# Two-input elementwise work moved from GpSimd to VectorE, high halves to ScalarE, in a hybrid attention layer

## Chip, cores and metric

The kernel runs on one core of a Trainium2 chip. The metric is device time in microseconds of one launch. TensorE, VectorE (DVE in the profile), ScalarE (ACT), GpSimd (POOL) and SyncE (SP, which issues the DMAs) each run their own instructions in order and wait for one another by semaphores.

## The reference, cut to what matters

One encoder layer over 2048 frames of 1024 features, in float32:

```python
h = layer_norm(x, ln_in_g, ln_in_b)
(aq, ak, av, ag, gq, gk, gv, gg, glr) = split(h @ w_in)
att = chunk_band_attention(aq, ak, av, rel_bias) * silu(ag)      # 8 heads x 64, 576-frame band
log_a = log_sigmoid(glr @ w_gla_gate + b_gla_gate) / 16
o = gla_chunked(gq, gk, gv, log_a)                               # 4 heads, dk 64, dv 128
gla = rms_normalised(o) * gla_norm_g * silu(gg)
r = alpha * h + concat(att, gla) @ w_out
r = r + sigmoid(r @ w_ple_gate + b_ple_gate) * (p @ w_ple)
out = layer_norm(r, ln_g, ln_b)
```

In the gated part, with `L` the running sum of `log_a` in a chunk of 64 frames, the kernel needs `q * exp(L)`, `k * exp(-L)`, `q * exp(-L)`, `k * exp(L)` and `k * exp(L_end - L)`.

## The kernel before

**Split operands.** Every large product is made of three matmuls: an operand is split into a high half (`hi`, the value rounded to the matmul's float32r) and a low half (`lo`, the value minus `hi`), and hi x hi, hi x lo and lo x hi are summed. So each of the 46 weight slabs used for the first time is loaded raw (128 x 1024, twice 128 x 1088), then split: a copy gives `whi`, a subtraction `wlo`. Halves that are used again in the second half of the sequence are stored to DRAM (`w_keep`, line 268) and fetched back. `ln_T` (line 220) splits the normalised, transposed input into `hh` and `hl`; `mix_split` (line 1133) splits the mixed heads into `mh` and `ml`. The helper `copy_split` (line 150) copies on VectorE and subtracts on an engine that its caller names.

**Stages.** The sequence is worked in two halves of 1024 frames (`sb`), each half in two groups of 512 (`g`). A half has a gated stage (`gla_phase`: projections and four gated units), an attention stage (`attn_phase`: four pairs of heads, 16 steps a pair and group) and an output stage (`out_phase`: output projection, embedding projection, gate, last normalisation). The second half has its weights fetched, so all weight splits are in the first half, between 10 and 611 us. The last normalisation of group 0 (`ln_out`) runs beside the gate's products; that of the second half's group 1 is `ln_last`.

**The order of the work** is written out by hand. `gemm` (line 302) issues 3 x 8 matmuls for one 128 x 512 result and calls `tick` after each four (after each eight in `gemm_v`). A tick runs what was put off to it: `defer(n, f)` puts `f` n ticks later in the list `pend`, or in `lazy` for weights. `set_side` adds a generator ("side") that is stepped beside the matmuls; each `yield w` lets `w` ticks pass, times the side's scale. `w_done(i)` (line 298) is called after the last matmul of weight i; one tick later `w_next(i + 4)` splits the weight four places on (high half on VectorE, low half on GpSimd) and starts the raw load two places further on. Raw weights have two buffers (three weights at the start have others), split ones eight, four weights' worth. Within what the dependencies allow, the framework lays out each engine's order; in the first stage (`head`, line 742) the order of VectorE, ScalarE and GpSimd is the program's own.

**The places the change touches.** `ln_T`: of the splits of full 512-column blocks, half have their subtraction on GpSimd (12 in all); the first group's half blocks have it on VectorE. `w_split` and `w_next` (lines 274 and 294): above. `ln_out` (line 370): per block of 128 frames two halves are scaled on VectorE (line 393) and get their bias added on GpSimd (line 395), 24 adds in all. `unit` (line 627), eight of them: after `gates` has made `eL`, `en`, `kd` and `kn`, VectorE makes `kd = kd * k`, GpSimd `qf`, and 1.5 ticks later TensorE transposes `kd` (line 639), ScalarE copies it out; VectorE makes `kn` in two steps (lines 642 and 645), GpSimd `qn` and `kf`. `head`: splits the first four weights in a written order. `mix_split`: 32 high halves on VectorE, the low halves half on VectorE and half on GpSimd. What stays on GpSimd in both kernels: the power in `rstd_of` (line 155), the scaling of the probabilities in `norm` (line 1002), `r_sum` (line 1191) and `ln_last`'s share.

Of the kernel before, what the change touches and what calls it, by code (L numbers as in the profile page):

```python
# [26 lines left out]
F32 = mybir.dt.float32  # L27
# [17 lines left out]
def hymba_layer_kernel(  # L45
# [174 lines left out]
    def ln_T(g, xs, pst, blocks=range(4)):  # L220
        c0 = blocks[0] * 128
        c = slice(c0, c0 + 128 * len(blocks))
        for k in range(8):
            ps = pst()
            for b in blocks:
                nc.tensor.transpose(ps[:, b * 128:(b + 1) * 128],
                                    xs[b][k // 4][:, (k % 4) * 128:(k % 4 + 1) * 128], ident)
            t = U("t")
            nc.scalar.activation(t[:, c], ps[:, c], AF.Identity, bias=lnb[:, k:k + 1], scale=lng[:, k:k + 1])
            if c0 == 0:  # L230
                hT_hi[k][g] = U("hh", F32R)
                hT_lo[k][g] = U("hl", F32R)
            copy_split(t[:, c], hT_hi[k][g][:, c], hT_lo[k][g][:, c],
                       nc.vector if k % 2 or len(blocks) < 4 else nc.gpsimd)
            yield
# [37 lines left out]

    def w_split(i, part=None):
        if i < len(order) and i not in wt and not first_use(i):
            w_fetch(i)
        if i not in wt or isinstance(wt[i], tuple) and len(wt[i]) == 2:
            return
        if part != "lo":
            raw = wt[i]  # L280
            hi = w_tile(pool_w, F32R, i, "whi")
            if part == "act":
                nc.scalar.activation(hi, raw, AF.Copy)
            else:
                nc.vector.tensor_copy(hi, raw)  # L285
            wt[i] = (raw, hi, None)
        if part in (None, "lo"):
            raw, hi, _ = wt[i]
            lo = w_tile(pool_w, F32R, i, "wlo")
            nc.gpsimd.tensor_tensor(lo, raw, hi.bitcast(F32), op=OP.subtract)  # L290
            wt[i] = (hi, lo)
            w_keep(i)

    def w_next(i):
        w_split(i)
        w_load(i + 2)

# [72 lines left out]
    def ln_out(sb, g, rows, ys, pst):  # L370
        for b in range(4):
# [20 lines left out]
            for hf in range(2):  # L392
                nc.vector.scalar_tensor_tensor(y[hf], y[hf], r[:, 0:1], rows[hf],  # L393
                                               op0=OP.mult, op1=OP.mult)
                nc.gpsimd.tensor_tensor(y[hf], y[hf], rows[2 + hf], op=OP.add)  # L395
                ln_put(sb, g, b, hf, y[hf])
# [110 lines left out]
    def gla_phase(sb):  # L507
# [119 lines left out]
        def unit(s, g, before):  # L627
# [6 lines left out]
            nc.vector.tensor_tensor(kd, kd, k, op=OP.mult)  # L634
            nc.gpsimd.tensor_tensor(qf, q, eL, op=OP.mult)
            yield 1.5
            p2 = ps_kv()
# [3 lines left out]
            nc.scalar.activation(kdT, p2, AF.Copy)  # L641
            nc.vector.tensor_tensor(kn[:, :, 0:3:2, :], c42(k), c42(en), op=OP.mult)
            nc.gpsimd.tensor_tensor(qn, q, en, op=OP.mult)
            yield 1.5
            nc.vector.tensor_tensor(kn[:, :, 1, :], kn[:, :, 1, :], c42(k)[:, :, 0, :], op=OP.mult)
            nc.gpsimd.tensor_tensor(kf, k, eL, op=OP.mult)
            yield 1.5

# [93 lines left out]
        def head(idx):  # L742
# [34 lines left out]
            with tc.manual_schedule(engines={E.DVE, E.Activation, E.Pool}):  # L777
# [10 lines left out]
                x_half(xs[1][1], r, nm, 0, nc.vector)  # L788
                w_split(0)
                for k, _ in enumerate(ln_T(0, xs, bank, range(0, 2))):  # L790
                    if k == 1:
                        w_split(1, "act")
                        w_split(1, "lo")
                w_split(2, "act")
# [338 lines left out]
    def mix_split(g):  # L1133
        for k in (4, 5, 0, 1, 2, 3, 6, 7):
# [3 lines left out]
            else:  # L1138
                ml[k][g] = U("ml", F32R)
            copy_split(mix[k][g], mh[k][g], ml[k][g], nc.gpsimd if k % 2 else nc.vector)  # L1140
            yield
# [208 lines left out]
```

## Time and profile before

| | |
|---|---|
| median of 3 runs | 1408.23 us (1406.45 to 1409.65) |
| the profiled execution | 1408.62 us |
| its span, first to last instruction | 1406.8 us |
| TensorE matmul | 96% of the span, 8440 matmuls |
| VectorE | 865.4 us, 62%, 1785 instructions |
| ScalarE | 552.3 us, 39%, 1126 instructions |
| GpSimd | 380.8 us, 27%, 355 instructions |
| mean granted clock of TensorE | 0.990 of full speed |
| DMA | 186.40 MB, 132 GB/s in the mean |

The span runs from the first instruction to the last; the execution's own time is 1.8 us longer. Matmuls follow one another in a pipeline, so a busy TensorE isn't one at its peak, but a gap in it is time in which no matmul ran. An engine's wait is put down to the instruction whose end released it. In a line of the time line, `[2.19 <-DVE hh L151]` means that the engine had been idle for 2.19 us and was released by VectorE's instruction of line 151 that writes `hh`.

### The profile page before, as it was taken

What the parts mean: (1) busy time and instruction counts of PE and PEld (TensorE: products, weight loads), DVE (VectorE), ACT (ScalarE), POOL (GpSimd) and SP (SyncE); (2) the same over time, 40 slices, a digit from 0 to 9 for tenths busy, and PEclk for the clock granted to TensorE, in tenths of its full rate; (3) what the DMA queues carried; (4) which work ended last, traced back from release to release, by engine and by line L of the source; (5) the groups of instructions that cost most, each with busy time, mean ns of one, the idle gap of its engine ahead of it and who ended that gap; (6) DMA issues with size and microseconds to landing.
All of it is one profiled execution on the core that took longest, in us unless ns stands there. A gap on an engine that the chain in (4) does not pass through costs nothing.

```text
span 1406.8 us, 22169 instructions
## 1 busy us (share of the span) xinstructions
PE 1348.1 (96%) x8440; PEld 1171.5 (83%) x8440; DVE 865.4 (62%) x1785; ACT 552.3 (39%) x1126; POOL 380.8 (27%) x355
## 2 busy tenths in 40 slices
PE   5879999999999999999999999999999999999985
PEld 5868888889988888788897888988998888888875
DVE  7674736666666976665875452666566668332286
ACT  4644414544454311414454542445454542112222
POOL 4251513232333432422462120121111123000052
PEclk9999999999999999999999999999999999999998
DMA  8360435241633335656613042421332213335551
GB/s 316 52 194 2 183 120 209 93 165 39 219 109 133 119 119 200 249 214 230 221 61 120 5 164 75 135 92 61 99 114 99 84 46 103 115 114 196 191 180 60
DMA packets 63442, 186.40 MB, mean 132 GB/s; under 512 B 7216, under 2 KB 9320, under 8 KB 63336
## 3 DMA queue, kind: packets, MB, share of 16 engines
q1 hardware_dynamic: 62816, 183.41, 37.1%
q10 hardware_dynamic: 520, 1.57, 1.0%
q8 instruction: 67, 1.10, 0.3%
q14 instruction: 39, 0.32, 0.1%
HBM read 119.28 MB, written 65.67 MB: 131 GB/s over the span
## 4 chain that ended last, share of the span: by engine, by line
PE 49%; DVE 6%; ACT 2%; issue 1%; POOL 1%; ACTq 0%; DVEq 0%; POOLq 0%
PE proj L313 32%; PE proj L912 3%; PE proj L553 3%; PE PV L1044 2%; PE PT L1024 2%; PE S L990 1%; PE S L988 1%; DVE t L1199 1%; DVE y L1205 1%; DVE ysb L393 1%; PE O L700 1%; DVE P L994 1%; DVE y L1207 0%; POOL ysb L395 0%; DVE bst L379 0%
## 5 line engine op out<-in xcount | busy, mean ns | idle before, releaser
L313 PE MATMUL proj<-hh,whi 128*128 128x512 f32 (+1 forms) x912 | 358.6, 393 | 0.3 <-DVE k L896 0.3
L313 PE MATMUL proj<-hh,wlo 128*128 128x512 f32 (+1 forms) x912 | 357.9, 392 | 0.0
L313 PE MATMUL proj<-hl,whi 128*128 128x512 f32 (+1 forms) x912 | 354.4, 389 | 0.0
L1006 POOL TENSOR_SCALAR P<-P,s 128x640 f32<-128x640 f32 (+4 forms) x128 | 96.0, 750 | 424.2 <-DVE s L1005 302.2
L313 PEld LDWEIGHTS proj<-hh,whi 128*128 128x128 f32 x912 | 172.9, 190 | 29.4 <-issue 1.0
L313 PEld LDWEIGHTS proj<-hl,whi 128*128 128x128 f32 x912 | 172.7, 189 | 29.6
L313 PEld LDWEIGHTS proj<-hh,wlo 128*128 128x128 f32 x912 | 172.7, 189 | 29.5
L998 ACT ACTIVATE P<-P,s 128x640 f32<-128x640 f32 (+4 forms) x128 | 97.6, 763 | 174.7 <-DVE s L997 150.9
L290 POOL TENSOR_TENSOR wlo<-wraw,whi 128x1024 fp32r<-128x1024 f32 (+1 forms) x46 | 111.3, 2418 | 134.4 <-DVE whi L285 78.3
L994 DVE CUSTOM_DVE_ANT_0 P<-S,bias 128x640 f32<-128x640 f32 (+4 forms) x128 | 94.5, 738 | 53.4 <-PE S L990 47.5
L1027 DVE TENSOR_TENSOR PTl<-PT,PTh 128x384 fp32r<-128x384 f32 (+2 forms) x232 | 102.4, 472 | 14.2 <-ACT PTh L1026 12.8
L313 PE MATMUL proj<-mh,whi 128*128 128x512 f32 x256 | 99.9, 390 | 0.0
L313 PE MATMUL proj<-mh,wlo 128*128 128x512 f32 x256 | 99.7, 389 | 0.0
L1026 ACT ACTIVATE PTh<-PT 128x384 fp32r<-128x384 f32 (+2 forms) x232 | 87.1, 421 | 27.4 <-PE PT L1024 26.3
L159 POOL TENSOR_TENSOR rstd<-v,nhalf 128x1 f32<-128x1 f32 (+2 forms) x44 | 35.6, 815 | 225.2 <-DVE v L157 224.5
L1024 PE MATMUL PT<-ident,P 128*128 128x128 f32 x560 | 84.1, 275 | 3.0 <-DVE PTl L1027 3.0
L553 PE MATMUL proj<-whi,hl 128*128 128x272 f32 (+1 forms) x256 | 76.5, 302 | 2.9 <-DVE hl L152 1.6
L553 PE MATMUL proj<-whi,hh 128*128 128x272 f32 (+1 forms) x256 | 75.5, 301 | 2.8 <-DVE hh L151 2.2
L313 PE MATMUL proj<-ml,whi 128*128 128x512 f32 x192 | 75.1, 391 | 0.0
L912 PE MATMUL proj<-whi,hh 128*128 128x256 f32 x256 | 74.3, 290 | 0.0
L1199 DVE SCALAR_TENSOR_TENSOR t<-t,ple 128x512 f32<-128x512 f32 (+1 forms) x36 | 39.8, 1107 | 53.2 <-ACT t L1198 53.1
L912 PE MATMUL proj<-wlo,hh 128*128 128x256 f32 x256 | 72.3, 282 | 0.0
(224 smaller groups left out, 2691.2 us busy)
## 6 DMA issues: line engine op xcount, KB each, us to landing
whi<-wkept SPq DMA_DIRECT2D x64, 512.0 KB, 3.7
wlo<-wkept SPq DMA_DIRECT2D x64, 512.0 KB, 4.5
wkept<-whi SPq DMA_DIRECT2D x44, 512.0 KB, 2.9
wkept<-wlo SPq DMA_DIRECT2D x44, 512.0 KB, 2.9
wraw<-in_wi_dram SPq DMA_DIRECT2D x26, 512.0 KB, 5.0
x<-in_x_dram SPq DMA_DIRECT2D x32, 256.0 KB, 5.8
out_dram<-ysb SPq DMA_DIRECT2D x32, 256.0 KB, 2.0
v<-vhist SPq DMA_DIRECT2D x24, 256.0 KB, 3.0
```

Of the source, the lines that this page charges most:

```text
L159: nc.gpsimd.tensor_tensor(r[:, :n], v1[:, :n], nhalf[:, :n], op=OP.pow)
L290: nc.gpsimd.tensor_tensor(lo, raw, hi.bitcast(F32), op=OP.subtract)
L313: nc.tensor.matmul(ps[:, cols], lhsT=l[:, c0 + k, :], rhs=rhs(k)[m][:, cols], start=(j == 0), stop=(j == n - 1))
L553: nc.tensor.matmul(ps[:, c0:c0 + nw], lhsT=h[k][g][:, b * 128:(b + 1) * 128], rhs=W[k // 4][m][:, k % 4, :], start=(n == 0), stop=(n == 23))
L912: nc.tensor.matmul(ps[:, bb * 256:bb * 256 + 256], lhsT=h[k][g][:, c], rhs=W[k // 4][m][:, k % 4, :], start=(k == 0 and n == 0), stop=(k = ...
L994: nc.vector.tensor_tensor_reduce(P[:, :ncol], ps[:, 512 - n_prev:512 + n_cur], bias[pr, h][:, 640 - ncol:640], 1.0, -3e38, OP.add, OP.max, ...
L998: nc.scalar.activation(P[:, :ncol], P[:, :ncol], AF.Exp, bias=s4[:, 1:2], scale=1.0, accum_out=s4[:, 2:3])
L1006: nc.gpsimd.tensor_scalar(P[:, :ncol], P[:, :ncol], s4[:, 3:4], 1.0, op0=OP.mult, op1=OP.mult)
L1024: nc.tensor.transpose(ps[:, b, :], P[:, (b0 + b) * 128:(b0 + b + 1) * 128], ident)
L1026: nc.scalar.activation(Th[:, ks, cs], ps[:, :nb, :], AF.Copy)
L1027: nc.vector.tensor_tensor(Tl[:, ks, cs], ps[:, :nb, :], Th[:, ks, cs].bitcast(F32), op=OP.subtract)
L1199: nc.vector.scalar_tensor_tensor(t, t, 1.0, ple[s][:, cols], op0=OP.add, op1=OP.mult)
```

## The change

GpSimd's subtractions and products with two tensor inputs in `ln_T`, `w_split`, `ln_out`, `unit` and `mix_split` go to VectorE. The high halves of weights, apart from the very first, and of the mixed heads are made on ScalarE. `w_next` makes the high half at once, and the low half and the next raw load two ticks later. In `unit` the transposes of `kd` come 2 ticks instead of 1.5 after its product, with `kn`'s two products issued in front of them and `qn` and `kf` behind. In `head` the first two low halves come after the splits of the first two blocks of input. The whole diff:

```diff
--- before.py
+++ after.py
@@ -231,7 +231,7 @@
                 hT_hi[k][g] = U("hh", F32R)
                 hT_lo[k][g] = U("hl", F32R)
             copy_split(t[:, c], hT_hi[k][g][:, c], hT_lo[k][g][:, c],
-                       nc.vector if k % 2 or len(blocks) < 4 else nc.gpsimd)
+                       nc.vector)
             yield
 
 
@@ -272,28 +272,32 @@
                 nc.sync.dma_start(d[n], w_flat(wt[i][n]))
 
     def w_split(i, part=None):
+
         if i < len(order) and i not in wt and not first_use(i):
             w_fetch(i)
         if i not in wt or isinstance(wt[i], tuple) and len(wt[i]) == 2:
             return
-        if part != "lo":
+        if not isinstance(wt[i], tuple):
             raw = wt[i]
             hi = w_tile(pool_w, F32R, i, "whi")
-            if part == "act":
+            if part == "dve":
+                nc.vector.tensor_copy(hi, raw)
+            else:
                 nc.scalar.activation(hi, raw, AF.Copy)
-            else:
-                nc.vector.tensor_copy(hi, raw)
             wt[i] = (raw, hi, None)
         if part in (None, "lo"):
             raw, hi, _ = wt[i]
             lo = w_tile(pool_w, F32R, i, "wlo")
-            nc.gpsimd.tensor_tensor(lo, raw, hi.bitcast(F32), op=OP.subtract)
+            nc.vector.tensor_tensor(lo, raw, hi.bitcast(F32), op=OP.subtract)
             wt[i] = (hi, lo)
             w_keep(i)
 
     def w_next(i):
-        w_split(i)
-        w_load(i + 2)
+        def rest():
+            w_split(i)
+            w_load(i + 2)
+        w_split(i, "act")
+        defer(2, rest, lazy)
 
     def w_done(i):
         del wt[i]
@@ -392,7 +396,7 @@
             for hf in range(2):
                 nc.vector.scalar_tensor_tensor(y[hf], y[hf], r[:, 0:1], rows[hf],
                                                op0=OP.mult, op1=OP.mult)
-                nc.gpsimd.tensor_tensor(y[hf], y[hf], rows[2 + hf], op=OP.add)
+                nc.vector.tensor_tensor(y[hf], y[hf], rows[2 + hf], op=OP.add)
                 ln_put(sb, g, b, hf, y[hf])
             yield
 
@@ -632,19 +636,19 @@
             eL, en, kd, kn, dA = gated.pop((s, g))
             qf, kf, qp, qn = (U(n) for n in ("qf", "kf", "qp", "qn"))
             nc.vector.tensor_tensor(kd, kd, k, op=OP.mult)
-            nc.gpsimd.tensor_tensor(qf, q, eL, op=OP.mult)
-            yield 1.5
+            nc.vector.tensor_tensor(qf, q, eL, op=OP.mult)
+            yield 2
+            nc.vector.tensor_tensor(kn[:, :, 0:3:2, :], c42(k), c42(en), op=OP.mult)
+            nc.vector.tensor_tensor(kn[:, :, 1, :], kn[:, :, 1, :], c42(k)[:, :, 0, :], op=OP.mult)
             p2 = ps_kv()
             for b in range(4):
                 nc.tensor.transpose(p2[:, b * 128:(b + 1) * 128], kd[:, b * 128:(b + 1) * 128], ident)
             kdT = U("kdT")
             nc.scalar.activation(kdT, p2, AF.Copy)
-            nc.vector.tensor_tensor(kn[:, :, 0:3:2, :], c42(k), c42(en), op=OP.mult)
-            nc.gpsimd.tensor_tensor(qn, q, en, op=OP.mult)
             yield 1.5
-            nc.vector.tensor_tensor(kn[:, :, 1, :], kn[:, :, 1, :], c42(k)[:, :, 0, :], op=OP.mult)
-            nc.gpsimd.tensor_tensor(kf, k, eL, op=OP.mult)
-            yield 1.5
+            nc.vector.tensor_tensor(qn, q, en, op=OP.mult)
+            nc.vector.tensor_tensor(kf, k, eL, op=OP.mult)
+            yield 1
 
 
             kv = ps_kv()
@@ -786,11 +790,12 @@
                 r, nm = next(st[1])
                 x_half(xs[1][0], r, nm, 0, nc.scalar)
                 x_half(xs[1][1], r, nm, 0, nc.vector)
-                w_split(0)
+                w_split(0, "dve")
                 for k, _ in enumerate(ln_T(0, xs, bank, range(0, 2))):
                     if k == 1:
                         w_split(1, "act")
-                        w_split(1, "lo")
+                w_split(0, "lo")
+                w_split(1, "lo")
                 w_split(2, "act")
                 st = [x_stat(xs, (b,)) for b in (2, 3)]
                 for _ in range(2):
@@ -1137,7 +1142,8 @@
                 ml[k][g] = pool_p.tile([128, 640], F32R, name="mlp", tag="p")[:, 0:512]
             else:
                 ml[k][g] = U("ml", F32R)
-            copy_split(mix[k][g], mh[k][g], ml[k][g], nc.gpsimd if k % 2 else nc.vector)
+            nc.scalar.activation(mh[k][g], mix[k][g], AF.Copy)
+            nc.vector.tensor_tensor(ml[k][g], mix[k][g], mh[k][g].bitcast(F32), op=OP.subtract)
             yield
```

## Rows read from the trace of the kernel before

**Rows 1.** The profile's page: the span, and each engine's busy time.

```profile
span 1406.8 us, 22169 instructions
...
PE 1348.1 (96%) x8440; PEld 1171.5 (83%) x8440; DVE 865.4 (62%) x1785; ACT 552.3 (39%) x1126; POOL 380.8 (27%) x355
```

**Rows 2.** TensorE's waits over the whole span: total us, times, longest us.

```profile
PE kvp L639 <- DVE kd L634: 10.6, 4, 4.1
PE O L226 <- ACT x L197: 10.3, 3, 8.8
PE tq L377 <- ACT ysb L388: 3.6, 2, 2.0
PE PT L1024 <- DVE PTl L1027: 3.0, 4, 1.8
...
PE proj L313 <- DVE t L1177: 2.6, 1, 2.6
...
PE tq L408 <- DVE y L1207: 2.2, 1, 2.2
...
PE O L680 <- POOL kf L646: 1.4, 1, 1.4
```

**Rows 3.** Time line of the start, by engine: start us, us, engine, line, operation [idle before].

```profile
10.55 2.48 POOL L290 TENSOR_TENSOR wlo<-wraw,whi 128x1088 fp32r<-128x1088 f32 x1 [0.99 <-DVE whi L285]
...
11.25 2.85 DVE L151 CAST hh<-t 128x256 fp32r<-128x256 f32 x1 [0.78 <-ACT t L229]
14.14 2.58 DVE L152 TENSOR_TENSOR hl<-t,hh 128x256 fp32r<-128x256 f32 x1
...
14.16 0.59 PE L553 MATMUL proj<-whi,hh 128*128 128x272 f32 x1 [2.19 <-DVE hh L151]
...
16.77 0.59 PE L553 MATMUL proj<-whi,hl 128*128 128x272 f32 x1 [1.59 <-DVE hl L152]
...
13.06 0.33 SPq L261 DMA_DIRECT2D wraw<-in_wi_dram  x1
```

**Rows 4.** Time line of VectorE and TensorE in two gated units.

```profile
99.61 0.96 DVE L607 TENSOR_TENSOR W<-L 128x4 f32<-128x4 f32 x1
...
100.57 1.50 DVE L615 TENSOR_TENSOR kn<-L 128x256 f32<-128x256 f32 x1
102.00 1.75 DVE L613 TENSOR_TENSOR kd<-W,L 128x512 f32<-128x512 f32 x1
...
105.34 0.90 PE L639 MATMUL kvp<-ident,kd 128*128 128x128 f32 x3 [4.12 <-DVE kd L634]
...
770.33 1.08 PE L639 MATMUL kvp<-ident,kd 128*128 128x128 f32 x4 [3.42 <-DVE kd L634]
```

**Rows 5.** Stretches: busy us (instructions) of PE, PEld, DVE, ACT, POOL; PEclk, DMA share, GB/s.

```profile
104.80:108.20 3.40, 2.86 (x14) 2.87 (x15) 1.02 (x3) 1.27 (x3) 0.00 (x0) 0.50 0.00 0
1367.70:1371.10 3.40, 3.40 (x18) 3.40 (x17) 1.43 (x7) 0.60 (x1) 0.00 (x0) 0.51 0.88 298
```

**Rows 6.** Single lines of the kernel: count, least/median/longest duration in ns, first and last start.

```profile
L290 POOL TENSOR_TENSOR wlo<-wraw,whi x46: 2351/2398/3195, 10.6 to 610.8; 128x1024 fp32r<-128x1024 f32 x44, 128x1088 fp32r<-128x1088 f32 x2
...
L285 DVE CAST whi<-wraw x43: 641/694/2887, 9.8 to 610.0; 128x1024 fp32r<-128x1024 f32 x42, 128x1088 fp32r<-128x1088 f32 x1
...
L283 ACT ACTIVATE whi<-wraw x3: 1042/1046/1106, 11.6 to 29.5; 128x1024 fp32r<-128x1024 f32 x2, 128x1088 fp32r<-128x1088 f32 x1
...
L634 DVE TENSOR_TENSOR kd<-kd,gk x8: 677/1414/1774, 71.4 to 824.9; 128x512 f32<-128x512 f32 x8
...
L645 DVE TENSOR_TENSOR kn<-kn,gk x8: 410/412/1510, 72.6 to 827.2; 128x256 f32<-128x256 f32 x8
```

**Rows 7.** Time line of VectorE and TensorE in the first output stage.

```profile
570.46 2.28 DVE L212 SCALAR_TENSOR_TENSOR nmr<-bmv,rstd 128x1 f32<-128x1 f32 x1
...
576.13 0.80 PE L313 MATMUL proj<-pTh,whi 128*128 128x512 f32 x1 [2.57 <-DVE t L1177]
```

**Rows 8.** Time line of VectorE near the end.

```profile
1338.21 1.60 DVE L1199 SCALAR_TENSOR_TENSOR t<-t,ple 128x512 f32<-128x512 f32 x1
```

## The prediction

> **What bounds the kernel now.** I read the page first: 1348.1 us of the 1406.8 us span is matmul, 96% [rows 1]. The 58.7 us without matmul is the most that moving elementwise work between engines can win, unless a wait also costs clock. So the second view is TensorE's own waits [rows 2]. The reader is to see how few they are. The 10.3 us on the first normalised rows is nearly all the 8.8 us of loading and statistics that opens the program, and stays. The 10.6 us on `kd` is four waits in the gated units. The others are 1 to 4 us each.
>
> The third view is the time line in front of these waits. At the start a GpSimd low half of a weight runs from 10.55 to 13.03; VectorE's cast of the first `hh` starts at 11.25 and takes 2.85 us, and the subtraction behind it 2.58 us beside the second GpSimd low half [rows 3]. Both end when the GpSimd instruction ends, and TensorE stands 2.19 and 1.59 us behind them. In the unit near 101 us a VectorE instruction on 256 columns takes 1.50 us and one on 512 columns 1.75 us, and TensorE waits 4.12 us; near 768 us TensorE waits 3.42 us behind `kd`'s own product [rows 4], which takes up to 1.77 us. Alone, the same shapes take 0.41 and 0.68 us (the least of each in [rows 6]). So each of TensorE's longer waits in the middle has a VectorE instruction in front of it that stood for a GpSimd one. The cost is the standing, not VectorE's load: 62% busy [rows 1].
>
> The fourth view is the granted clock. Right behind the 4.12 us wait TensorE has 0.50 of full speed, the 1.2 GHz level, for 3.4 us, and 0.51 behind a 2.2 us wait near 1366 us [rows 2, 5]. Such a stretch does half of its work: it costs 1.7 us. There are five of them before the last 12 us (from 104.8, 575.8, 770.4, 1354.1 and 1367.7 us), each behind a wait of over 2 us.
>
> **The change, part by part.** The sum is made against the profiled execution, 1408.62 us, which is 0.4 us above the median of the three runs; the difference is under a measurement's uncertainty, about 0.2% (2.8 us).
>
> *Prices.* VectorE with two SBUF inputs takes 0.41 us for 256 and 0.68 us for 512 columns [rows 6], so 0.27 us per 256 more; a low half of 1024 columns is then about 1.22 us (estimate), against 2.40 us on GpSimd. ScalarE's high half is 1.05 us where VectorE's takes 0.69 us [rows 6].
>
> *Start.* The two blocked instructions go back to 0.28 us and 0.43 us (estimates from the 256-column minimum 0.41 us, and the cast's own rate, 0.64 us for 1024 columns): 4.7 us of VectorE time, and TensorE's 3.8 us of waiting with it. In return both low halves (2 x 1.25 us) stand on VectorE between the transposes' splits and the statistics of the next two blocks, and two more behind those; the first low half now ends some 5 us later, and with it the third raw load on SP's queue, which went at 13.06 us once GpSimd's low half was done [rows 3], and the eight x loads behind it. I take 3.8 us of gain and 1.5 us of loss for the statistics; ends: 5 us gain, 1.7 us loss (the 5.5 us by which the loads move, less 3.8).
>
> *Gated units.* Three GpSimd products per unit (24) go to VectorE at 0.68 us. Near 101 us the blocked pair loses (1.50 - 0.41) + (1.75 - 0.68) = 2.2 us, and the blocked tiny sum in front of it (0.96 us on four columns [rows 4]) some 0.7; one moved product stands in front, +0.68; the transposes come half a tick later, which lets about 0.5 us of other matmuls go first (a tick is four wide or eight narrow matmuls, about 1 us): 4.12 shrinks by 2.7 us. Near 768 us two steps in front of the transposes lose up to 1.1 us each (1.51 - 0.41 and 1.77 - 0.68 [rows 6]), so by the same count 3.42 shrinks by 2.0. The other two, 3.1 us in all of the 10.6, lose 1.4 (half a tick each and a little more). That is 6.1 us, and the two low-clock stretches behind the two long waits, 2 x 1.7. The wait on GpSimd's `kf`, 1.4 us [rows 2], goes too; what is late next there is VectorE's `kf` at 0.68 us, so I take 1.0. Ends for all this: 2 us (three products in front of `kd`) and 15.4 us (12.0 of waits and 3.4 of clock).
>
> *Weights.* 42 high halves go to ScalarE (44 us there, 39% busy [rows 1]) and 46 low halves to VectorE. A high half waits for its buffer, which TensorE frees, and for its raw load; behind it on ScalarE stand the evacuations and the exponentials, and TensorE waits for those two matmul groups later, which covers 1 us. Cover is thin in the gated stage, where one chain of ScalarE and VectorE steps leads to `kd`: ten casts and ten low halves, of which I let one in five fall into the chain: 10 x (1.05 + 1.22) / 5 = 4.5 us of loss. Ends: 0 and 22.7. The low half, its two stores to DRAM and the raw load two weights on come two ticks (2 us) later on SP's queue; weights are split four ahead of their use, which hides it, and without that cover it would be 2 us a weight.
>
> *Output stage, first half.* At 570.46 us a one-column VectorE instruction takes 2.28 us beside a GpSimd low half, and 5.7 us later TensorE resumes after a 2.57 us wait [rows 7]. Gone: 2.1 us and the 0.69 us cast, added 1.22: the wait shrinks by 1.6, and without it the low-clock stretch goes, 1.7 us. Together 3.3; ends 0 and 4.3.
>
> *Mixed heads.* 32 high halves to ScalarE, 16 low halves to VectorE, in the tails of both attention stages where TensorE waits 3.0 us on `PTl` [rows 2]. I take 1.0; ends -1 and 3.
>
> *Last normalisation's adds.* 24 adds go to VectorE. Per block, two GpSimd adds hold VectorE's 512-column steps at 1.60 us [rows 8] instead of 0.68; three steps would be 2.8 us a block, and I take 2.4, since the adds cover only part of the third; two adds of 0.68 us come in, and the `r_sum` that stays on GpSimd still blocks once, 1 us. 2.4 against 2.4: nothing, with ends of -5 and +7.6 (the two last waits of 2.0 and 2.2 us with their clock stretches). The 12 low halves of `ln_T` cost 0.68 us each on VectorE, beside TensorE's matmuls, and stand at nothing; uncovered they would be 8 us.
>
> Sum: 3.8 - 1.5 + 6.1 + 3.4 + 1.0 - 4.5 + 3.3 + 1.0 + 0 = 12.6 us. 1408.6 - 12.6 = 1396.0; against the median, 0.4 us less, **1395.6**.
>
> **The rivals.** *More is won:* the last stage gains too, as its waits of 2.0 and 2.2 us and their two clock stretches go (7.6 us): 1388. For it: both waits follow blocked steps. Against: the adds come back on the same engine. 0.10.
>
> *No change:* VectorE takes on 46 x 1.22 + 76 x 0.68 = 108 us and gives away 42 x 0.69 + 32 x 0.41 = 42, so it gains 66 us of work, about what the blocked time loses; if the order of VectorE puts the new work where the standing was, the waits stay: 1406 to 1411. 0.08.
>
> *VectorE becomes the units' bound (slower):* `kd` queues behind all three moved products in all eight units, 8 x 3 x 0.68 = 16.3 us, and each of the six units that now has no low-clock stretch gets one (6 x 1.7 = 10). Without the units' gain, and with the other terms (3.8 - 1.5 + 3.3 + 1.0 - 4.5 = 2.1): 1408.6 - 2.1 + 16.3 = 1423, up to 1433 with the clock. It decides where `kd`'s exponential comes later than the three products could have run, so they go first. Against it: `kd` stands ahead of them in the program. 0.07.
>
> *ScalarE holds TensorE up (slower):* each of the 26 casts made in the gated and attention stages delays an evacuation or exponential that TensorE is about to need, 26 x 1.05 = 27 us, in place of the 4.5 and against 17.1 of gain: 1408.6 - 17.1 + 27 = 1418.5. For it: ScalarE is slower at this copy, 1.05 against 0.69 us [rows 6], and VectorE has room. The Trainium skill ("Perfetto Trace Analysis", Optimizing Scalar/DVE Operations) says that an operation with a fast VectorE mode is quicker there and that moving it to ScalarE may pay where VectorE is saturated; at 62% it isn't, so by that rule this part would be a loss. Against it: ScalarE has 61% idle and TensorE waits little for it in the middle. 0.07.
>
> **How the numbers follow.** The forecast's own case has 0.68 (1388 to 1404). With "more is won" that is 0.78 for faster by over 0.2%. Same: 0.08. Slower: the two rivals, 0.14. The range leaves out about half of "more is won" and of the forecast's tail below 1385, and the two slower rivals above 1410: 1385 to 1410.
>
> **What would show it.** Right: no VectorE instruction of 256 to 512 columns at 1.3 us or more before 1300 us; `hh` at the start under 0.5 us; TensorE's waits on `kd` under 5 us in all; no low clock near 105, 576 and 770 us; GpSimd under 200 us busy (46 x 2.4 = 110 us go with the low halves alone, and 76 two-input instructions of 512 columns with them), ScalarE near 615 (42 x 1.05 and 32 at about 0.6 more). Wrong: waits of TensorE on ScalarE's `qh`, `PTh` or `kdT` that weren't there, or `kd` waits of over 10 us.

## The result, and the profile after

The changed kernel takes **1384.86 us** (median of four runs, 1382.27 to 1387.53) against 1407.59 (1406.45 to 1409.65): ratio 0.983, 95% interval 0.982 to 0.985. It is 22.7 us faster; the forecast was 12.6, and its range began at 1385.0. The profiled run took 1383.77, its span 1381.9.

The page's span and busy times after the change, which answer to [rows 1]:

```profile
span 1381.9 us, 22143 instructions
...
PE 1339.8 (97%) x8440; PEld 1166.5 (84%) x8440; DVE 829.1 (60%) x1833; ACT 609.7 (44%) x1200; POOL 154.0 (11%) x233
```

TensorE is busy 8.3 us less, though it has the same matmuls: nearly all of that is clock got back, some 2.5 us in the first 23 us and 4.9 in the stretches of half clock behind them, both below. VectorE is busy 36 us less, though by the forecast's own count it has 66 us more work: about 100 us of standing (time in which an instruction runs longer than the same shape does alone) went. GpSimd gave up 227 us, ScalarE took on 57. TensorE's waits over the whole span, as in [rows 2]:

```profile
PE O L226 <- ACT x L197: 11.0, 4, 9.2
PE kvp L645 <- DVE kd L638: 3.3, 3, 2.6
PE tq L412 <- DVE bst L414: 2.6, 1, 2.6
PE tq L412 <- DVE y L1213: 2.5, 1, 2.5
PE CN L317 <- ACT whi L286: 2.2, 1, 2.2
PE tq L412 <- DVE y L1208: 2.0, 1, 2.0
...
PE PT L1029 <- DVE PTl L1032: 0.8, 2, 0.4
```

The waits on `kd` fell from 10.6 to 3.3 us; those on `t` (2.6) and on GpSimd's `kf` (1.4) left the list, `ysb` fell from 3.6 to 0.4 and `PTl` from 3.0 to 0.8. New is 2.2 us on a high half that ScalarE makes (`whi`). The three on `bst` and `y` belong to the last stage and were there before, at 2.6, 2.2 and 2.0 us.

The lines that answer to [rows 6] (count; least, median, longest ns; first and last start), three steps of the gated units last:

```profile
L291 DVE TENSOR_TENSOR wlo<-wraw,whi x46: 1198/1226/1284, 17.5 to 597.1; 128x1024 fp32r<-128x1024 f32 x44, 128x1088 fp32r<-128x1088 f32 x2
...
L286 ACT ACTIVATE whi<-wraw x45: 1042/1061/1107, 12.0 to 596.0; 128x1024 fp32r<-128x1024 f32 x44, 128x1088 fp32r<-128x1088 f32 x1
...
L638 DVE TENSOR_TENSOR kd<-kd,gk x8: 684/693/694, 66.7 to 804.2; 128x512 f32<-128x512 f32 x8
...
L641 DVE TENSOR_TENSOR kn<-gk,en x8: 685/688/693, 65.5 to 804.9; 128x512 f32<-128x512 f32 x8
...
L642 DVE TENSOR_TENSOR kn<-kn,gk x8: 417/420/421, 67.3 to 806.1; 128x256 f32<-128x256 f32 x8
```

Least and longest are now nearly the same: in [rows 6] the unit's 512-column step went from 677 to 1774 ns, the 256-column step from 410 to 1510. Counted over the time line up to 1300 us, VectorE had 64 instructions of 1.3 us or longer before, and has one now, at 9.67 us beside a GpSimd memset.

The low-clock stretches near 105, 576, 770 and 1354 us are gone, a new one stands at 28 us, and that of 1367.7 us is now at 1342.1, behind the same wait on `y`. TensorE worked 16.2 us in the five stretches of before and 6.5 in the two of after, so half of the difference, 4.9 us, is won (columns as in [rows 5]):

```profile
28.00:31.40 3.40, 3.40 (x17) 3.40 (x17) 3.08 (x8) 2.38 (x8) 0.00 (x0) 0.50 1.03 410
104.80:108.20 3.40, 3.40 (x32) 2.78 (x27) 2.19 (x5) 3.02 (x6) 0.00 (x0) 1.00 0.02 5
1342.10:1345.50 3.40, 3.04 (x14) 3.04 (x15) 1.87 (x7) 0.60 (x1) 0.00 (x0) 0.50 0.00 0
```

At the start the 1.2 GHz level also ends earlier: the same matmul of 128 x 272 still takes 0.43 us at 21.60 us before, and only 0.29 at 15.83 us after (two lines of before, then two of after):

```profile
21.60 0.43 PE L553 MATMUL proj<-whi,hh 128*128 128x272 f32 x1
22.94 0.29 PE L553 MATMUL proj<-whi,hh 128*128 128x272 f32 x1
...
13.78 0.43 PE L557 MATMUL proj<-whi,hl 128*128 128x272 f32 x1
15.83 0.29 PE L557 MATMUL proj<-whi,hl 128*128 128x272 f32 x1
```

TensorE works 9.6 us at that level before (to 22.9 us) and 4.4 us after (to 14.3 us), so some 2.5 us are won there.

**Where the gain arises.** I compared, for the n-th projection matmul, its start after the change with its start before. TensorE is 5.8 us ahead at 22 us (time of before), only 0.5 at 32 and 0.9 at 41, then 3.0 at 50 and 4.8 at 62, 7.3 at 82, 10.1 at 108 (the first units), falls back to 7.2 at 434 (attention), is 9.7 ahead at 477, 14.0 at 579 (output stage, first half), 15.9 at 736, 20.6 at 774 (units of the second half), 21.8 at 1169 and at 1330, and 25.0 at 1358; the span is 24.9 shorter.

### The profile page after: what moved, and what is told of

It is laid out like the page before. It is cut to its first block, busy times and chain, and to the rows that moved or that the text cites. A ratio compares the mean times of both kernels' runs of the same rounds, so it can differ in the third digit from the quotient of the medians.

```text
span 1381.9 us, 22143 instructions
## 1 busy us (share of the span) xinstructions
PE 1339.8 (97%) x8440; PEld 1166.5 (84%) x8440; DVE 829.1 (60%) x1833; ACT 609.7 (44%) x1200; POOL 154.0 (11%) x233
## 4 chain that ended last, share of the span: by engine, by line
PE 81%; DVE 8%; ACT 5%; issue 2%; DMA 2%; POOL 1%; SPq 0%; ACTq 0%; DVEq 0%; POOLq 0%
PE proj L317 51%; PE proj L917 7%; PE proj L557 4%; PE PV L1049 4%; PE PT L1029 4%; PE S L995 2%; PE S L993 2%; DMA wraw<-in_wi_dram 1%; PE O L704 1%; DVE P L999 1%; ACT P L1003 1%; DVE PTl L1032 1%; ACT whi L286 1%; DVE wlo L291 1%; ACT qh L885 1%
## 5 line engine op out<-in xcount | busy, mean ns | idle before, releaser
L1029 PE MATMUL PT<-ident,P 128*128 128x128 f32 x560 | 84.5, 275 | 1.0 <-DVE PTl L1032 0.8
L291 DVE TENSOR_TENSOR wlo<-wraw,whi 128x1024 fp32r<-128x1024 f32 (+1 forms) x46 | 56.1, 1225 | 46.6 <-ACT whi L286 44.8
L917 PE MATMUL proj<-whi,hl 128*128 128x256 f32 x256 | 72.4, 283 | 0.0
```

The lines of the kernel that those rows point to most:

```text
L291: nc.vector.tensor_tensor(lo, raw, hi.bitcast(F32), op=OP.subtract)
L917: nc.tensor.matmul(ps[:, bb * 256:bb * 256 + 256], lhsT=h[k][g][:, c], rhs=W[k // 4][m][:, k % 4, :], start=(k == 0 and n == 0), stop=(k = ...
L1029: nc.tensor.transpose(ps[:, b, :], P[:, (b0 + b) * 128:(b0 + b + 1) * 128], ident)
```

## The experiments

Each is the changed kernel with one part undone, or something added. "Lowest" is the best of its runs. Each was timed against the kernel before on the same chip, on four chips, with medians between 1408.61 and 1409.01, so that the runs can be set against e1.

| run | edit | median (range), us | against e1: median / lowest | ratio to before, interval |
|---|---|---|---|---|
| e1 | after, as it is | 1384.84 (1383.59 to 1388.5) | 0 | 0.983 (0.982 to 0.985) |
| e2 | last adds back | 1388.78 (1387.44 to 1393.91) | +3.9 / +3.9 | 0.986 (0.984 to 0.987) |
| e3 | low halves of `ln_T` back | 1386.47 (1384.48 to 1387.71) | +1.6 / +0.9 | 0.984 (0.983 to 0.986) |
| e4 | units back | 1396.05 (1394.73 to 1397.3) | +11.2 / +11.1 | 0.991 (0.990 to 0.992) |
| e5 | weights' low halves back | 1387.77 (1386.29 to 1391.94) | +2.9 / +2.7 | 0.986 (0.984 to 0.988) |
| e6 | weights' high halves back | 1383.9 (1383.23 to 1385.3) | -0.9 / -0.4 | 0.983 (0.981 to 0.984) |
| e7 | mixed heads back | 1388.03 (1384.18 to 1390.83) | +3.2 / +0.6 | 0.985 (0.982 to 0.987) |
| e8 | half a tick back | 1389.14 (1388.25 to 1390.84) | +4.3 / +4.7 | 0.986 (0.985 to 0.988) |
| e9 | weights wholly back | 1389.92 (1388.07 to 1392.38) | +5.1 / +4.5 | 0.987 (0.985 to 0.988) |
| e10 | ballast, two inputs | 1387.67 (1386.54 to 1390.89) | +2.8 / +3.0 | 0.986 (0.984 to 0.987) |
| e11 | ballast, one input | 1383.85 (1382.81 to 1385.28) | -1.0 / -0.8 | 0.983 (0.981 to 0.984) |
| e12 | fourth raw load free | 1385.44 (1382.41 to 1388.17) | +0.6 / -1.2 | 0.984 (0.982 to 0.986) |
| e13 | heads' odd low halves back | 1385.41 (1384.77 to 1386.07) | +0.6 / +1.2 | 0.983 (0.982 to 0.985) |
| e14 | e12 and e6 | 1384.32 (1379.58 to 1386.31) | -0.5 / -4.0 | 0.982 (0.980 to 0.983) |
| e15 | e14 and last stage on VectorE | 1380.85 (1379.02 to 1385.18) | -4.0 / -4.6 | 0.980 (0.979 to 0.982) |

The lowest stands beside the median because of one thing that falls into some executions and not into others. In four of the sixteen profiles (e2, e7, e9, e14) TensorE stops near 75 to 80 us, before the same matmul (the last five of the first gated unit), with no releaser. In e7:

```profile
74.22 0.28 PE L684 MATMUL O<-qn,kf 64*64 64x64 f32 x3
79.35 0.34 PE L684 MATMUL O<-qn,kf 64*64 64x64 f32 x5 [4.86 <-issue]
```

It is 4.8 to 4.9 us in three of them and 3.3 in e9, and a low-clock stretch follows (0.58 from 80.5 to 84.5 us in e2). An execution that holds it is longer by that much; of the executions that left no trace it can't be told, so a median may hold it or not.

A queue that fetches instructions (q8; 67 packets of 16 KB in every run) goes with the stall. In each of the 13 profiles without it, the one of the kernel before among them, one of its packets starts between 61 and 67 us. In the four with it none starts between 56 and 75 us; the next one comes inside the stall, which ends about 1.5 us after that packet has landed (in e7 it runs from 76.97 to 77.85 us, and TensorE goes on at 79.35). The instruction packets from 56 to 70 us, in e1 and then in e7:

```profile
q8 instruction: 1, 0.02, 0.6%
q14 instruction: 1, 0.01, 0.1%
...
q14 instruction: 1, 0.01, 0.1%
```

So TensorE most likely ran out of instructions there. That is read from 17 profiles and not tested, and why the packet comes late stays open.

**e1, the base.**

> The changed kernel as it is, as the measure for the runs beside it: 1385 us by both theories (median before 1384.86).

It repeats the result, so what follows is compared with it.

**e2, the last normalisation's adds.**

```diff
-                nc.vector.tensor_tensor(y[hf], y[hf], rows[2 + hf], op=OP.add)
+                nc.gpsimd.tensor_tensor(y[hf], y[hf], rows[2 + hf], op=OP.add)
```

> The 24 adds of ln_out go back to GpSimd, all else as changed. Theory A (each GpSimd instruction with tensor inputs makes VectorE stand, and TensorE pays wherever VectorE leads to it): 4 to 5 us slower than the changed kernel, 1389 to 1390, since the matmul sequence gained 1.5 us beside the first half's and 3.2 us beside the second half's normalisation; the low clock near 1354 us comes back. Theory B (the forecast's term: two adds in, one standing out, nothing): 1385, within 1 us.

3.9 slower: not nothing. The time lines of VectorE and TensorE in e2 near the end, and the windows behind:

```profile
1347.19 1.76 DVE L1205 SCALAR_TENSOR_TENSOR t<-t,ple 128x512 f32<-128x512 f32 x1
1348.99 1.63 DVE L1211 SCALAR_TENSOR_TENSOR y<-t,hh 128x512 f32<-128x512 f32 x1
...
1337.73 0.66 PE L381 MATMUL tq<-ident,y 128*128 128x128 f32 x4 [2.03 <-ACT ysb L392]
...
1351.40 0.48 PE L412 MATMUL tq<-ident,y 128*128 128x128 f32 x1 [3.28 <-DVE y L1213]
...
1350.20:1353.60 3.40, 2.19 (x10) 2.20 (x11) 2.68 (x8) 0.60 (x1) 0.00 (x0) 0.51 0.76 214
1353.60:1357.00 3.40, 3.40 (x17) 3.40 (x17) 0.89 (x4) 0.74 (x2) 0.00 (x0) 0.50 0.44 178
```

With the adds on VectorE (e1) the two steps take 0.68 and 0.69 us, the wait on `ysb` 0.39 instead of 2.03, that on `y` 2.46 instead of 3.28, and the low clock behind it lasts 3.4 us instead of 6.8. That is 1.6 + 0.8 + 1.7 = 4.1 us, which agrees with the 3.9 (the 1.7 of clock is the least sure: e4, e9 and e15 have the same wait on `y`, 2.44 to 2.47 us, and no low clock behind it); TensorE's start against e1 falls back by 4.0 between 1328 and 1349 us, so the stall near 75 us, which this profile has too, is no part of it.

**e3, the low halves of `ln_T`.**

```diff
-                       nc.vector)
+                       nc.vector if k % 2 or len(blocks) < 4 else nc.gpsimd)
```

> The 12 low halves of ln_T go back to GpSimd. Theory A: 3 to 4 us slower, most of it between 45 and 62 us and some between 680 and 705 us. Theory B (forecast: beside TensorE's matmuls, nothing): within 1 us of the changed kernel.

1.6 slower (0.9 by the lowest), under the theory's 3 to 4 and over the forecast's nothing. Beside GpSimd's subtraction the next cast stands, 1.25 us for 0.42:

```profile
51.76 1.28 POOL L152 TENSOR_TENSOR hl<-t,hh 128x512 fp32r<-128x512 f32 x1 [1.42 <-DVE hh L151]
...
51.27 0.42 DVE L151 CAST hh<-t 128x512 fp32r<-128x512 f32 x1
52.08 1.25 DVE L151 CAST hh<-t 128x512 fp32r<-128x512 f32 x1 [0.40 <-ACT t L229]
```

**e4 and e8, the units.** e4 puts back the whole unit, e8 only the time of the transposes (`yield 2` to `yield 1.5` behind `qf`).

> The gated unit as before the change: qf, qn and kf on GpSimd, transposes after 1.5 ticks, the old order. Theory A: 8 to 10 us slower, the low clock near 100 and 750 us back. Theory B (the forecast's gain of 6.1 + 3.4 + 1.0 less 4.5 for the weights' instructions in this chain, so 10.5 from this part alone): 10.5 us slower. A third reading, that the weights' low halves on GpSimd made the unit's instructions stand, and not its own products: under 3 us slower.

> The units as changed, but with the transposes half a tick earlier (1.5 ticks after kd's product instead of 2). Theory A (only the standing mattered): within 1 us. Theory B (the forecast counted 0.5 us for each of the four units that waited): 2 us slower, and up to 3.7 with one low-clock stretch.

e4 costs 11.2, against 10.5 in the forecast. TensorE's waits on `kd` are 11.7 us in all, and three low-clock stretches are back:

```profile
PE kvp L643 <- DVE kd L638: 11.7, 4, 3.5
...
69.00:72.40 3.40, 3.40 (x13) 2.65 (x12) 3.40 (x5) 0.67 (x2) 0.55 (x1) 0.63 0.59 101
100.40:103.90 3.50, 2.85 (x14) 2.85 (x15) 2.54 (x4) 0.60 (x1) 1.72 (x2) 0.53 0.00 0
763.00:766.40 3.40, 3.40 (x19) 3.40 (x18) 0.00 (x0) 1.06 (x2) 0.00 (x0) 0.53 0.00 0
```

e8 alone costs 4.3: with the transposes half a tick earlier TensorE reaches them before `kd` is there in the first unit (a wait of 2.07 us at 68.67 instead of 0.20 at 68.25 in e1), and clock goes with it: 0.55 from 69.3 to 72.7 and 0.54 from 100.1 to 103.5 us, where e1 has full clock. Only the first of the two has a longer wait in front of it: that of the second is 2.42 us in e8 and 2.53 in e1, and e11 and e13, which keep the two ticks, have that stretch too (from 98.1 and 98.4 us). The theory that half a tick is worth at most 1 us is wrong: some 4 of the 11 us are the move; if the two add up, the rest is the three products and the old order of the steps, which e4 puts back as well.

**e5, e6 and e9, the weights.** e5 puts the 42 low halves of `w_next` back on GpSimd, e6 their high halves on VectorE, e9 both with the old start and the old single step.

```diff
-            nc.vector.tensor_tensor(lo, raw, hi.bitcast(F32), op=OP.subtract)
+            (nc.vector if i < 4 else nc.gpsimd).tensor_tensor(lo, raw, hi.bitcast(F32), op=OP.subtract)
```

```diff
-        w_split(i, "act")
+        w_split(i, "dve")
         defer(2, rest, lazy)
```

> The low halves of all weights but the first four go back to GpSimd (42 subtractions of 2.4 us), the high halves stay on ScalarE, the timing of two ticks later stays. Theory A (GpSimd's reading makes VectorE stand): 6 to 9 us slower than the changed kernel (1384.84), with the wait on ev_r near 560 us back (4.6 us with its low clock) and more in the gated stage and at the end of the attention stage. Theory B (the forecast's terms: 3.3 us in the output stage, less 10 x 1.22 / 5 = 2.4 us that the low halves were to cost on VectorE): 0.9 us slower.

> The 42 high halves of weights made on VectorE again (0.69 us), low halves on VectorE too, timing as changed. Theory A: no matter, within 1.5 us, since nothing of this size made TensorE wait. Theory B (the forecast's ScalarE loss, 10 x 1.05 / 5 = 2.1 us, against 10 x 0.69 / 5 = 1.4 on VectorE): 0.7 us faster. The rival by which ScalarE's casts hold TensorE up: up to 27 us faster less what VectorE's cost, and in any case over 3 us faster, most of it in the attention stage, where the changed kernel's matmuls fell 3.3 us behind between 190 and 430 us.

> Everything about the weights as before (high halves on VectorE, low halves on GpSimd, both made in one step, and the start's old order); units, mixed heads, low halves of the rows and last adds as after. The forecast's terms for this part are start +2.3, output stage +3.3, weights -4.5: 1.1 us slower than after, about 1386. The two half undos gave +2.9 (low halves on GpSimd) and -0.9 (high halves on VectorE); if they simply add, +2.0, about 1387. Theory of standing: a high half on VectorE beside a low half on GpSimd stands for it, which neither half undo had, so more than the sum: +3 to +6, 1388 to 1391, with the 2.2 us stand near 570 us and the low-clock stretch behind it back.

The move of the weights was to cost 4.5 us beside what it wins at the start and in the output stage; with those it was to win 1.1. Undone as a whole it costs 5.1 (4.5 by the lowest), though the halves undone one by one make only 2.9 - 0.9 = 2.0. Part of the surplus may be the 3.3 us stall of e9's profile; the lowest runs, 4.5 against 2.3, say that most of it is not. The two half undos keep the new order of the start, and e9 doesn't: its trace is 2.8 us behind e1 at 62 us, before the stall, which is about the surplus. In e9's output stage VectorE stands for the low half on GpSimd, and TensorE waits 2.46 us:

```profile
566.02 2.39 POOL L290 TENSOR_TENSOR wlo<-wraw,whi 128x1024 fp32r<-128x1024 f32 x1
...
571.39 2.40 POOL L290 TENSOR_TENSOR wlo<-wraw,whi 128x1024 fp32r<-128x1024 f32 x1 [1.90 <-issue]
...
566.16 2.27 DVE L212 SCALAR_TENSOR_TENSOR nmr<-bmv,rstd 128x1 f32<-128x1 f32 x1
...
571.80 2.53 DVE L1180 SCALAR_TENSOR_TENSOR t<-hl,t 128x512 f32<-128x512 f32 x1
...
571.83 0.50 PE L313 MATMUL proj<-pTh,whi 128*128 128x512 f32 x1 [2.46 <-DVE t L1178]
```

e6 decides the rival on ScalarE: with its 42 casts back on VectorE the time falls by 0.9 at most, so having them on ScalarE costs about 1 us net and not 27. In e6's trace TensorE gains 1.7 us on e1 between 86 and 374 us and gives back 1.5 near 564.

**e7 and e13, the mixed heads.** e7 restores `copy_split(..., nc.gpsimd if k % 2 else nc.vector)`; e13 leaves the high halves on ScalarE and puts the 16 low halves of odd k on GpSimd.

> The mixed heads split as before (high halves on VectorE, every second low half on GpSimd). Theory A, by the matmul sequences of the two kernels: 3 to 3.6 us slower (2.4 us near 460 to 477 us, 1.2 us near 1160 to 1190). Theory B (the forecast): 1.0 us slower.

> After, with the low halves of the mixed heads of odd k back on GpSimd (16 instructions); their high halves stay on ScalarE. Theory of standing: most of what the mixed heads undone cost is the GpSimd low halves, beside which VectorE stands: 1 to 3 us slower than after, 1386 to 1388. Rival (the 4.9 us stall of TensorE without a releaser near 75 us, in the profile of the undone one, is what its median shows, and the heads are worth only the forecast's 1.0, half of it high halves): within 1 us of after, 1384 to 1386.

e7's median is 3.2 over, but its profile holds the 4.9 us stall, and its lowest run is 0.6 over. Where its edit acts, its trace falls behind e1's by 1.0 us between 434 and 477 us and by 1.1 between 1130 and 1190. e13, with no stall, is 0.6 over, the lowest 1.2; where its edit acts its trace loses 0.2 and 0.2, and the 1.5 us by which it is behind at 154 us can't come from it. So this part is worth 1 to 2 us against 1.0 forecast, and the GpSimd low halves alone make little of it: in e7 the casts stand beside them, up to 1.52 us for 0.41.

**e10 and e11, ballast in the units.** GpSimd computes in each unit three products that nobody reads, into the unused end of `kn`'s buffer; in e11 each is two one-input instructions instead. From the edit of e10:

```diff
+            nc.gpsimd.tensor_tensor(scr, k, eL, op=OP.mult)
...
+            nc.gpsimd.tensor_tensor(scr, q, en, op=OP.mult)
...
+            nc.gpsimd.tensor_tensor(scr, qf, qf, op=OP.mult)
```

> After, and in each of the eight gated units GpSimd computes three products of 512 columns that nobody reads, into an unused part of kn's buffer, where before had its three. Theory of standing (VectorE waits while GpSimd reads two inputs, whoever needs the result): VectorE's products of the unit stand up to 1.5 or 1.8 us again, TensorE waits for kd again, 4 to 9 us slower than after (units undone cost 11.2, of which the half tick is 4.3): 1389 to 1394. Rival, lateness (what cost was that the results came late from a slow engine): nobody waits for these, so within 1 us of after, 1384 to 1386.

> As the ballast of two inputs, but each product is two one-input operations of the same 512 columns (about the same time of GpSimd). If only two-input reading makes VectorE stand (as the one-input normalisation of P beside VectorE suggests, which showed no longer instructions), within 1 us of after, 1384 to 1386. If any GpSimd work beside VectorE costs, as much as with two inputs, 1389 to 1394.

This is the run that separates standing from lateness, since nobody waits for these results. Two inputs cost 2.8 us in the median: less than the theory's 4 to 9, but not the 0 of lateness. (The profiled execution, 1390.89, is the slowest of its four, and its span is 6.6 us over e1's.) No engine waits for the ballast, but TensorE's waits on `kd` are 6.6 us instead of 3.2, and VectorE, with the same instructions, is busy 851.0 us instead of 828.8. Lines of e10 (the wait; then count; least, median, longest ns):

```profile
PE kvp L647 <- DVE kd L639: 6.6, 4, 2.1
...
L639 DVE TENSOR_TENSOR kd<-kd,gk x8: 679/693/1775, 68.8 to 811.2; 128x512 f32<-128x512 f32 x8
...
L643 DVE TENSOR_TENSOR kn<-gk,en x8: 680/1358/1784, 65.9 to 811.8; 128x512 f32<-128x512 f32 x8
...
L644 DVE TENSOR_TENSOR kn<-kn,gk x8: 410/1259/1509, 69.4 to 815.2; 128x256 f32<-128x256 f32 x8
```

and of e11:

```profile
L639 DVE TENSOR_TENSOR kd<-kd,gk x8: 686/693/1101, 67.0 to 805.4; 128x512 f32<-128x512 f32 x8
...
L644 DVE TENSOR_TENSOR kn<-gk,en x8: 692/895/1108, 65.8 to 806.0; 128x512 f32<-128x512 f32 x8
...
L645 DVE TENSOR_TENSOR kn<-kn,gk x8: 418/828/839, 67.7 to 808.1; 128x256 f32<-128x256 f32 x8
```

The same 256-column step takes 418 ns alone, 828 in the middle beside one-input work, 1259 beside two-input work; the 512-column step at most 1.1 and 1.8 us. So one-input work makes VectorE stand too, up to 0.4 us an instruction, which I had not expected; VectorE is busy 843.7 us in e11. TensorE's waits on `kd` stay at 3.5 us, and no cost shows in the median (1.0 under e1). The pair is not a clean one: e11's first pair reads `k` alone and starts at 57.0 us in the first unit, where e10's product waits for `eL` until 65.4, so the two ballasts fall beside different VectorE steps. The rows that e11's expectation leaned on are of VectorE steps with one input in PSUM: before, `PTl` on 384 columns takes 0.56 us in the middle beside the normalisation of P and without GpSimd. The unit's steps have both inputs in SBUF.

The Trainium skill ("SBUF — State Buffer", Who interferes with whom) says that a VectorE instruction with two SBUF inputs contends with a GpSimd instruction that reads SBUF. The direction agrees with these rows. That the loser blocks for the whole instruction it says of VectorE's two-port modes, not of two inputs; here, beside e11's one-input instructions of 0.80 to 1.12 us in the middle, the 256-column step's median lengthens by 0.41, so the whole is not lost each time.

**e12, e14 and e15, a better version.** e12 gives the fourth raw load a buffer of its own; e14 adds e6; e15 also moves the last five GpSimd products of `ln_last` (1361 to 1375 us in e12) to VectorE.

```diff
-    w_load(3)
+    w_load(3, pool_t, "t")
...
-        fin(0, 1, nc.gpsimd)
-        fin(0, 0, nc.gpsimd)
+        fin(0, 1, nc.vector)
+        fin(0, 0, nc.vector)
...
-        fin(1, 0, nc.gpsimd, nc.gpsimd)
+        fin(1, 0, nc.vector)
...
```

> After, with the fourth weight's raw load in a buffer of its own, so that it goes to the queue without waiting for the first low half. Theory: in after this load waits on SP behind the late low half, TensorE waits 2.2 us for its high half and has a 3.4 us low-clock stretch behind it (1.7 us): 3 to 4 us faster than after, 1381 to 1382. Rival (another wait of the start takes its place, the rows of x or the second block's statistics): within 1 us, 1384 to 1385.

> After with two edits together: the fourth raw load in its own buffer, and the 42 high halves on VectorE. Alone they gave, in medians, +0.6 (with 2.0 less in the profiled span) and -0.9. If both gains add: 1381 to 1383. Rival (both act on the same early waits, or the difference is under what the medians tell): 1384 to 1385.

> As the run before, and the last stage's five remaining GpSimd products of 512 columns on VectorE. Theory of standing: near 1365 us four VectorE instructions of 256 columns take 1.4 us beside them instead of 0.42; that is 3.3 us won, and five products of 0.68 us, 3.4, come in, two of which go where VectorE stood 0.65 us each in the tail: within 1 us of the run before, 0.5 faster at best. Rival (the standing is free at the end because TensorE waits for other things): 2 to 3 us slower than the run before.

After the change the fourth raw load goes late, behind eight loads of x and two stores (SP's queue, ScalarE and TensorE at the start of after):

```profile
16.95 1.26 SPq L272 DMA_DIRECT2D wkept<-whi  x2
18.86 0.33 SPq L261 DMA_DIRECT2D wraw<-in_wi_dram  x1
...
26.70 1.06 ACT L286 ACTIVATE whi<-wraw 128x1024 fp32r<-128x1024 f32 x1 [1.74 <-DMA wraw<-in_wi_dram]
...
27.81 0.44 PE L317 MATMUL CN<-hh,whi 128*128 128x256 f32 x1 [2.25 <-ACT whi L286]
```

In e12 that wait is 0.40 instead of 2.25 us, but the low-clock stretch stays (0.52 from 26.8 to 30.2 us): the clock fell there without the long wait. In e14, with the same edit and the same 0.40 us, it doesn't fall. The profiled span is 2.0 shorter than e1's, but e11, with the start as it was, is 1.7 us ahead of e1 at 35 us too, so the start's own scatter is as large; the median is 0.6 higher. e14's profile holds the stall, and its lowest run is 4.0 under e1's. e15 is the fastest of all in median, 1380.85, though its interval still touches that of e1. VectorE near 1365 us, two of four steps in after and then in e15:

```profile
1365.29 0.71 DVE L1205 SCALAR_TENSOR_TENSOR t<-t,ple 128x256 f32<-128x256 f32 x1
...
1367.33 1.48 DVE L1205 SCALAR_TENSOR_TENSOR t<-t,ple 128x256 f32<-128x256 f32 x1
```

```profile
1364.29 0.42 DVE L1205 SCALAR_TENSOR_TENSOR t<-t,ple 128x256 f32<-128x256 f32 x1
...
1365.08 0.42 DVE L1205 SCALAR_TENSOR_TENSOR t<-t,ple 128x256 f32<-128x256 f32 x1
```

The four steps, 0.71 to 1.48 us in after, are back to 0.42. The lowest runs of e15 and e14 are 0.6 us apart, as the theory had it, since five products come in. So e15 is 4.0 us under the changed kernel in the median, which the touching intervals leave short of shown. Its trace, 5.4 us shorter than e1's, is 1.4 ahead at 35 us, wins 2.7 between 86 and 374 us (e6's wins 1.7 there) and gives back 1.2 near 564, wins 1.5 near 1344, where the wait on `y` is 2.47 us as in e1 but no low clock follows, and only 1.1 behind 1352 us, where the moved products are.

## Why the prediction was right, and where it was wrong

| part of the sum | forecast gain | undone: median / lowest |
|---|---|---|
| start, weights, output stage (3.8 - 1.5 - 4.5 + 3.3) | 1.1 | 5.1 / 4.5 |
| gated units (6.1 + 3.4 + 1.0) | 10.5 | 11.2 / 11.1 |
| mixed heads | 1.0 | 3.2 / 0.6 |
| last normalisation's adds | 0 | 3.9 / 3.9 |
| low halves of `ln_T` | 0 | 1.6 / 0.9 |
| sum | 12.6 | 25.0 / 21.0 |

e1 is 24.2 us under its kernel before, so the parts make up the whole.

- **What bounds the kernel: right.** TensorE's waits behind standing VectorE instructions, and the clock behind them, were the cost. The ballast shows that standing costs though nobody waits for GpSimd's result.
- **Gated units: right in kind, and in sum**: 7.3 us of waits on `kd` went for 6.1 forecast, and both clock stretches. The shares are others: the wait near 105 us was to shrink from 4.12 to 1.4 and is still 2.58 (at 97.94 us). VectorE no longer stands in front of it; it waits for ScalarE's exponentials (1.35 us for `en`, 0.50 for `kd`), which the forecast had not counted. That no low clock follows it is luck: in e11 and e13 it does, behind 2.38 and 2.70 us. The half tick was undersized: 0.5 us of matmuls in each of the four units that waited was counted for it, 4.3 us were measured, waits and the clock behind them.
- **Weights: wrong, the largest miss.** "One in five fall into the chain: 10 x (1.05 + 1.22) / 5 = 4.5 us of loss" did not happen: with the low halves back on GpSimd, e5 loses 1.9 us between 99 and 153 us instead of winning, and e6 puts ScalarE's share at about 1. That new work was charged to VectorE without the standing that goes was the error: the 1.22 us low half takes the place of a stand of up to 1.8 us for the instruction beside it.
- **Output stage: right in kind**, 3.3 forecast; TensorE gains 4.3 us there between 477 and 579 us.
- **Start: right in sum, partly by luck.** `hh` fell to 0.28 us and TensorE was 5.8 us ahead at 22 us, more than the 3.8, since the clock rises earlier too, which the term left out. The loss was 5.3 instead of 1.5, so at 32 us only 0.5 was left; but the old start's wait of 1.74 us on x at 43 us went as well, and at 50 us the lead is 3.0 for 2.3 forecast. The step named what would be late, the third raw load on SP's queue, but not the high half behind it nor the clock. One reading was loose: the first cast of `hh` ended at 14.10 us, 1.07 after the low half, and at the end of two GpSimd memsets (13.96), so a one-input step can stand for a memset as well (in after, the step at 9.67 us takes 1.49 us beside one, and 0.54 at 8.48 us).
- **Mixed heads: right in kind**, 1.0 forecast and 1 to 2 measured.
- **Last adds: wrong, 0 forecast and 3.9 measured.** "2.4 against 2.4: nothing" balanced VectorE's time per block and left out which step ends in front of a wait of TensorE. The rival "more is won" had the mechanism, and half of its 7.6 us came: the wait on `ysb` (2.0) went with its clock stretch, the wait on `y` stayed (2.2 before, 2.5 after) with its own.
- **Low halves of `ln_T`: nothing forecast, 0.9 to 1.6 measured.** They are covered on VectorE, as said; what was left out is that on GpSimd they made the next cast stand.
- **The rivals.** "VectorE becomes the bound" didn't occur: the `kd` product takes 0.69 us in all eight units. "ScalarE holds TensorE up" is the 1 us of e6, with the new `whi` wait at the start. "No change" is out.
- **The signs.** All but one hold: `kd` waits 3.3 (under 5), GpSimd 154 (under 200), ScalarE 610 (615), `hh` 0.28 (under 0.5), no low clock near 105, 576 and 770 us; one VectorE instruction over 1.3 us against none.

In short, the miss of 10 us lies in three terms: the weights (4.5 of loss that did not come), the last adds (0 for 3.9) and the low halves of `ln_T` (0 for 0.9 to 1.6). In the first and the third the standing that goes was left out, though the same prediction had named standing as the cost (in the first the new work was charged beside it); in the second it was counted, but per block and not at the step for which TensorE waits. Some of each number is chance: a like wait has a low-clock stretch behind it in one execution and none in another.

## What to carry to other kernels

Where GpSimd's two-input work runs beside VectorE's, count for each GpSimd instruction what VectorE stands beside it, and set that against the short time the same work takes on VectorE; busy time alone says nothing of it. A wait of TensorE is worth more than its length where a low-clock stretch stands behind it, which changes from execution to execution, so a small move of the waiting step (half a tick) can be worth as much as the work that is moved. When a low half goes later, look at the queue in which the next load waits for its buffer.

## What was not expected of the hardware

- One-input GpSimd work lengthens VectorE's steps by up to 0.4 us (e11), two-input work by up to 1.1 us (e10).
- The clock does not follow the length of one wait: 2.58 us at 95.4 us in after leaves it at full, while in e12 it falls to 0.52 at 26.8 us behind a wait of 0.40 us (two of 0.76 and 0.64 us and a thin stretch stand in front). Nor does it fall each time: the wait on `y` between 1340 and 1355 us is 2.44 to 2.47 us in after, e1, e4, e9, e14 and e15, with low clock behind it in after, e1 and e14 alone.
- TensorE can stop for 3.3 to 4.9 us with no releaser, always before the same matmul, in some executions only; an instruction packet comes late in each of them, and why is open.
